# A gated-delta-net stage in a four-layer decoder kernel: projections in another order, PSUM banks given out by their last readers, weight parts given a higher rank

## The chip, the cores and the metric

The kernel runs on one core of a Trainium2 chip. The metric is the device time of one launch in microseconds (us).

## The reference, cut to what matters

A prompt of 512 tokens and 8 samples of 8 tokens (64 more) go through four layers: GLA, gated DeltaNet (GDN), S5, GLA. Each layer projects its input `x` (1024 wide), mixes over tokens with a recurrent state, gates with a SiLU branch, projects back and applies a LayerNorm to the residual sum. The change lies in the second layer:

```python
def gdn_mixer(x, w_in, w_conv, a_log, dt_bias, norm_g, w_out, conv0, s0):
    h = jnp.einsum('bld,de->ble', x, w_in).astype(F32)
    qkv, z, a, b = jnp.split(h, [...], axis=-1)
    ext = jnp.concatenate([conv0.astype(F32), qkv], axis=1)
    conv = ext[:, 0:L] * wc[0]
    for t in range(1, GDN_CONV):
        conv = conv + ext[:, t:t + L] * wc[t]
    q, k, v = jnp.split(jax.nn.silu(conv), [GDN_KW, 2 * GDN_KW], axis=-1)
    q = l2_normalize(...) * GDN_DK ** -0.5
    k = l2_normalize(...)
    g = -jnp.exp(a_log) * jax.nn.softplus(a + dt_bias)
    o, s = gdn_chunked(q, k, v, g, jax.nn.sigmoid(b), s0)
    o = rms_head(o, norm_g) * jax.nn.silu(z.reshape(bt, L, GDN_HEADS, GDN_DV))
    out = jnp.einsum('ble,ed->bld', o.reshape(bt, L, GDN_VW), w_out)
```

`gdn_chunked` needs only q, k and the gates for its scores and its triangular solve; v enters after the solve, z after the heads' outputs. There are 8 heads of width 128; the kernel works on pairs of heads, p = 0 to 3.

## The kernel before, in words

**The order is made by a planner in the kernel's own Python.** The code is written as threads (generators), each with a rank: low goes first. Every engine call is recorded (`record`, line 254) with its dependencies and a modelled cost (`cost`, 328). `run` (548) advances a model clock; on each engine it issues, of the operations that are ready in the model, the one of lowest rank (`issue`, 385). The order of issue is the program's order on that engine. On the chip each engine works through this order strictly, with real waits.

**Ranks.** The dense thread (all projections, in one list) has rank 10. What reads a finished projection out of PSUM has rank 1. Mixers have 3 and more: the thread of head pair p has 3 + p, its scores 2.5 + p, its heads 3 + p, its sample part 4.5 + p. Weight splitting has rank 5.

**Weights.** A unit of weights is 128 x 1024 words (512 KB), loaded by one SyncE DMA into one of RAW = 3 buffers (`load_weights`, 668). `split_weights` (687) makes a high part (a cast, on ScalarE or VectorE) and a low part (a VectorE subtraction) in one of RING = 4 buffers (line 142); a unit that is projected by `fm` (735) costs 48 matmuls of 288 columns: 8 slices of K, 2 token halves, 3 products of high and low parts. `prefetch` (681) splits a unit only when fewer than 4 units are held ahead of the dense thread, and when its load has landed.

**The dense thread** (`dense`, 705) takes the units strictly in the order of its list. `gdn_items` (1296) gives it for the GDN layer: the gates' unit and k, q of pair 0 (five units), then by line 1330

```python
        for w in 'v0 k1 k2 k3 v1 z0 z1 z2 v2 v3 z3'.split():
```

where `kN` is four units (k and q of two heads) and `vN`, `zN` are two. The out-projection (8 units, `out_items`, 827) follows; then the S5 layer.

**What a unit needs before its first matmul.** PSUM: `fm` takes two neighbouring banks of the eight (`bank(2)`, 465). SBUF: for a k, q or v unit `gdn_space` (1335) allocates 600 + 597 + 27 words a partition of convolution room, and a k unit (for itself and its q) 1024 words, a v unit 512, a z unit 576 (`gdn_zspace`, 1349). The pool has 32,960 words a partition. The dense thread must also leave `self.reserve` = 2500 words free (1301), a pair's thread 2000 until the pair before it is wholly done (1305). A thread that doesn't get its room waits, and with the dense thread all units behind it.

**After a k, q or v unit**, `gdn_conv` (1419): two copies out of PSUM, a scaling on ScalarE, three VectorE multiply-adds of 600 columns, one DMA of the convolution's last rows to `out_conv`, two SiLUs. After a z unit: one ScalarE SiLU of 576 columns.

**A pair** (`gdn_pair`, 1458) waits until pair p - 1 has passed its scores and pair p - 2 its solve; then scores (transposes, squares, matmuls, `gdn_scores`, 1632), one DMA to the scratch `scr`, a solve in 31 dependent VectorE steps (`gdn_solve`, 1615) that ends with one VectorE stream transpose, the heads (`gdn_head`, 1676; each ends with a DMA to `out_p_gdn` and waits for its v on the way), and the gate (`gate`, 1289), which waits for z, multiplies and hands the pair's output to the out-projection. A pair gives back its k, q, v and score buffers at the ends of its heads, its outputs and z only behind the gate.

**Banks.** `bank` takes the first free bank by its model time; a bank counts as free from `free` (489) on, that is once the reading instruction has been recorded, whether it has been issued or not. `bank_free` holds the model time of that call.

Of the kernel before, what the change touches and what calls it, by code (L numbers as in the profile page):

```python
# [184 lines left out]
class Core:  # L185
# [142 lines left out]
    def cost(self, op, method, args, kw, outs, ins):  # L328

        eng = op.eng  # L330
        column = any(v.shape[-1] == 1 for v in ins) or len(outs) > 1
        if not outs:
            op.cost, op.table = 1.28, args[0]
            return
        out = outs[0]
        size = lambda v: prod(v.shape[1:])
        n = size(out) if eng == 'PE' else max(size(v) for v in outs + ins)
        if eng == 'PE':
            m = 0.111 * size(ins[0]) / P
            if method == 'transpose':  # L340
                op.cost = max(n * 0.867e-3, 0.06)
            elif kw['lhsT'].dtype == F32R:
                op.cost = max(8e-3 + n * 0.434e-3, m)
            else:
                op.cost = 2 * max(n * 0.843e-3, m, 0.055)
        elif eng == 'DVE':
            in_ps = any(v.tensor.name == self.ps_name for v in outs + ins)
            op.cost = 0.07 + n / 960.0 * (0.5 if not in_ps and method in ('tensor_copy', 'tensor_scalar') else 1)
            if column:
                op.cost += 0.06  # L350
        elif eng == 'ACT':
            sb = all(v.tensor.name != self.ps_name for v in ins)
            op.cost = 0.05 + 0.835e-3 * n + (0.043 if sb else 0.0) + (0.093 if column else 0.0)
            op.table = ACT_SETS.get(args[2] if len(args) > 2 else None)
        elif eng == 'POOL':
            op.cost = 0.3 + 0.165 * n if kw.get('op') == ALU.pow else 0.12 + 2.2e-3 * n
            if method == 'memset':
                op.cost = 0.1 + 0.6e-3 * n
        else:
            run = min(self.run_of(v) for v in outs + ins)  # L360
            op.cost, op.tail = 0.45, prod(out.shape) / run * (8e-3 + 0.188e-3 * run) / 16
# [23 lines left out]
    def issue(self, op):  # L385
        e = op.eng
        t = max(self.now, op.ready)
        if e == 'PE' and not self.granted(t):
            op.cost *= 2
            self.pending[e] += op.cost / 2  # L390
        if op.table is not None:
            sets = op.table if isinstance(op.table, tuple) else (op.table,)
            if self.table not in sets:
                self.table = sets[0]
                if isinstance(op.table, tuple):
                    t += 1.28
        self.clock[e] = t + op.cost
        op.end = t + op.cost
        if e == 'SP':
            self.dma = max(self.dma, op.end + 0.7) + op.tail  # L400
            op.end = self.dma + 1.0
        op.issued = True
        self.pending[e] -= op.cost
        if e == 'PE' and op.rank >= 10:
            self.dense_backlog -= 1
        fn, args, kw = op.call
        fn(*args, **kw)  # L407
        op.call = None
        for s, lat in op.succ:
            s.ready = max(s.ready, t if lat is None else op.end + lat)  # L410
            s.pend -= 1
            if not s.pend:
                heappush(self.queue[s.eng][0], (s.ready, s.seq, s))
        op.succ = None

    def writers(self, *aps):
        ids = set()
# [46 lines left out]

    def bank(self, n=1, held=None):

        while True:
            best = None
            for b in range(0, 8, n):
                if held is not None and all({c, c + 1} & {b, *held} for c in range(0, 8, 2)):  # L470
                    continue
                if not any(self.banks[b:b + n]):
                    t = max(max(self.bank_free[b:b + n]), self.now)
                    key = (t, not self.banks[b ^ 1] if n == 1 else 0)
                    if best is None or key < best[0]:
                        best = (key, b)
            if best is None:
                yield BLOCK
                continue
            b = best[1]  # L480
            self.banks[b:b + n] = [True] * n
            if held is not None:
                held.append(b)
            v = self.ps[:, 512 * b:512 * (b + n)]
            return v if n == 1 else v.rearrange("p (a n) -> p a n", a=n)

    bank_free = [0.0] * 8

    def free(self, *aps):
        for v in aps:  # L490
            if v.tensor.name == self.ps_name:
                b, n = v.offset // 512, prod(v.shape[1:]) // 512
                self.banks[b:b + n] = [False] * n
                self.bank_free = list(self.bank_free)
                self.bank_free[b:b + n] = [self.now] * n
            else:
                off = v.offset
                n = self.used.pop(off)
                self.holes.append([off, n])
                self.holes.sort()  # L500
                merged = []
                for o, s in self.holes:
                    if merged and merged[-1][0] + merged[-1][1] == o:
                        merged[-1][1] += s
                    else:
                        merged.append([o, s])
                self.holes = merged
        self.frees += 1
# [39 lines left out]
    def run(self):  # L548
        while True:
            wake = []  # L550
            moved = True
            while moved:
                moved, wake = False, []
                for th in list(self.threads):
                    c = self.can_go(th)
                    if c is not True:
                        if c is not False:
                            wake.append(c)
                        continue
                    self.cur = th  # L560
                    moved = True
                    try:
                        v = next(th[0])
                    except StopIteration:
                        self.threads.remove(th)
                        continue
                    if v is BLOCK:
                        v = self.frees
                    elif isinstance(v, bass.AP):
                        v = self.writers(v)  # L570
                    elif isinstance(v, list):
                        v = self.writers(*v)
                    th[3] = v
                for e in ENGINES:
                    waiting, ready = self.queue[e]
                    while waiting and waiting[0][0] <= self.now + 1e-9:
                        _, s, op = heappop(waiting)
                        heappush(ready, (op.rank, s, op))
                    if ready and self.clock[e] <= self.now + 1e-9:
                        self.issue(heappop(ready)[2])  # L580
                        moved = True
# [15 lines left out]
class Kernel(Core):  # L597
    def __init__(self, ctx, tc, a, o, layers):
# [22 lines left out]
        self.reserve = 0  # L621
        self.xres = {}
        self.loaded = self.split = self.done = 0
        self.flat = []


    def load(self, dst, name, src=None):
# [53 lines left out]
    def prefetch(self, limit=1):  # L681
        self.load_weights(RAW)
        while limit and self.split < min(self.loaded, self.done + RING) and self.written(self.raw[self.split % RAW]):
            self.split_weights()
            limit -= 1

    def split_weights(self):
        cur, self.cur = self.cur, [None, 5] + self.cur[2:]
        src, lowrank = self.flat[self.split]
        raw, wh, wl = self.raw[self.split % RAW], self.wh[self.split % RING], self.wl[self.split % RING]  # L690
        for cs in self.pieces(self.split):
# [8 lines left out]
            else:  # L700
                self.TT(l, r, h.bitcast(F32), ALU.subtract)
        self.cur = cur
        self.split += 1

    def dense(self, items):

        for srcs, body in items:
            need = self.done + len(srcs)
            while self.split < need:
                self.prefetch(8)  # L710
                if self.split < need:
                    if self.split == self.loaded:
                        yield [self.raw[self.split % RAW]]
                    self.split_weights()
            idx = [i % RING for i in range(self.done, need)]
            ws = [(self.wh[i], self.wl[i]) for i in idx]
            for v in body(ws):
# [109 lines left out]
    def out_items(self, layer, wname):  # L827
# [9 lines left out]
        def half0(ws):  # L837
            ps, held = {}, []
            for u in range(4):
# [4 lines left out]
                for t in order:  # L844
# [6 lines left out]
                    if u == 3:  # L851
                        self.go(self.out_evac(layer, st, t, 0, ps[t]), 1)
                self.done += 1

        def half1(ws):
            for t in order:
                ps = yield from self.bank()
                for kt in range(KT):
# [3 lines left out]
                    if kt % 2:  # L862
                        yield
                        self.done += t == 3
                self.go(self.out_evac(layer, st, t, 1, ps), -1 if t == 3 and layer == self.layers - 1 else 0)

        w = self.a[wname]
# [428 lines left out]
    def gdn_items(self, layer):  # L1296
# [30 lines left out]
            return [([], body)]  # L1327

        items = [([], begin), self.fm_first(layer, first[:3])] + fms(first[3:])
        for w in 'v0 k1 k2 k3 v1 z0 z1 z2 v2 v3 z3'.split():  # L1330
            p = int(w[1])
            items += fms(kq(p)) if w[0] == 'k' else {'v': v, 'z': z, 'g': gate}[w[0]](p)
        return items
# [1017 lines left out]
```

## Time and profile before

| | us |
|---|---|
| median of 3 runs | 1349.48 |
| lowest and highest run | 1342.3, 1353.95 |
| the profiled execution | 1351.13 |
| its span, first to last instruction | 1349.3 |
| mean granted clock of TensorE in the span | 0.974 |

Nearly all instructions go through one recording line (407), so the profile shows no lines of the source; an instruction is told by its engine, operation, shape and buffers: `fx` is the fixed buffer (x and split weights), `sb` the working memory, `ps` PSUM. A matmul `ps<-fx` of 128x288 is a projection by `fm`; of 128x512 one of an out-projection. `ps<-sb` is mixer work. `PE` is TensorE, `DVE` VectorE, `ACT` ScalarE, `SP` SyncE, which issues the DMAs. A clock of 1.00 is 2.4 GHz, 0.5 is 1.2 GHz. By the weight loads the first GLA layer ends and GDN begins at about 300 us; GDN ends at about 750, S5 at about 1050.

### The profile page before, as it was taken

The page shows a single profiled execution, that of the slowest core. Times are in us where ns is not written, and L with a number is a line of the kernel's source. Part 1 is how long each engine was busy: PE and PEld are TensorE (multiplying, and loading weights), DVE is VectorE, ACT ScalarE, POOL GpSimd, SP SyncE. Part 2 cuts the span into 40 slices and gives each one's busy share as a digit, 9 for nine tenths or more (in the row PEclk, how much of TensorE's full clock was granted, in tenths as well). Part 3 has the DMA queues.
Part 4 walks back from the last instruction along what each step waited for, and adds up shares of the span by engine and source line. Part 5 has one row for each costly group of instructions (what it writes and reads, how often), then busy time and mean ns, then how long its engine had stood idle before and what let it go on. Part 6 is the DMA issues. An engine that isn't in the chain of part 4 may idle for free. (4 is left out here: it accounts for less than half of the span.)

```text
span 1349.3 us, 23532 instructions
## 1 busy us (share of the span) xinstructions
PE 1269.1 (94%) x8795; PEld 1185.0 (88%) x8795; DVE 960.1 (71%) x2099; ACT 599.2 (44%) x1329; POOL 152.6 (11%) x303
## 2 busy tenths in 40 slices
PE   8899999998998785999999989999999999999997
PEld 8898889778997685999977989899998899999986
DVE  5897887899999698786667729255334876655557
ACT  5553444423957663644541324235213245443430
POOL 5510010011111130121101000000000200000001
PEclk9999999999998897999989999899999999999999
DMA  7236444725367626263463697854325333332341
GB/s 237 67 114 207 145 161 149 244 86 173 105 171 225 173 68 182 86 180 107 120 206 102 250 264 199 227 147 106 95 87 176 113 111 99 129 130 98 121 152 70
DMA packets 129537, 198.35 MB, mean 147 GB/s; under 512 B 47176, under 2 KB 85960, under 8 KB 127376
## 3 DMA queue, kind: packets, MB, share of 16 engines
q1 hardware_dynamic: 129424, 196.86, 48.2%
q8 instruction: 69, 1.13, 0.4%
q14 instruction: 44, 0.36, 0.1%
HBM read 153.64 MB, written 47.37 MB: 149 GB/s over the span
## 5 line engine op out<-in xcount | busy, mean ns | idle before, releaser
L407 PE MATMUL ps<-fx 128*128 128x288 f32 (+2 forms) x6736 | 1053.6, 313 | 17.4 <-DVE sb L407 10.3
L407 PEld LDWEIGHTS ps<-fx 128*128 128x128 f32 x6736 | 953.9, 191 | 67.0 <-DVE sb L407 9.0
L407 DVE TENSOR_TENSOR fx<-sb,fx 128x1024 fp32r<-128x1024 f32 (+5 forms) x308 | 252.9, 847 | 168.2 <-ACT fx L407 164.6
L407 ACT CAST fx<-sb 128x1024 fp32r<-128x1024 f32 (+5 forms) x311 | 222.3, 741 | 314.0 <-PE ps L407 263.7
L407 PE MATMUL ps<-sb 128*128 128x128 f32 (+10 forms) x2059 | 301.0, 295 | 54.6 <-ACT sb L407 22.0
L407 PEld LDWEIGHTS ps<-sb 128*128 128x128 f32 (+7 forms) x2059 | 249.2, 177 | 88.7 <-ACT sb L407 28.6
L407 DVE TENSOR_TENSOR sb<-sb 128x128 f32<-128x128 f32 (+29 forms) x667 | 265.5, 415 | 13.9 <-ACT sb L407 4.8
L407 ACT COPY sb<-ps 128x512 f32<-128x512 f32 (+9 forms) x240 | 94.5, 413 | 132.8 <-PE ps L407 68.0
L407 DVE SCALAR_TENSOR_TENSOR sb<-sb 128x600 f32<-128x600 f32 (+6 forms) x205 | 134.0, 662 | 15.2 <-POOL sb L407 6.6
L407 ACT ACTIVATE sb<-sb 128x128 f32<-128x128 f32 (+9 forms) x240 | 108.1, 501 | 64.0 <-DVE sb L407 61.7
L407 DVE SCALAR_TENSOR_TENSOR sb<-sb,ps 128x256 f32<-128x256 f32 (+3 forms) x216 | 92.9, 458 | 59.3 <-PE ps L407 46.2
L407 POOL TENSOR_TENSOR sb<-sb 128x1 f32<-128x1 f32 (+4 forms) x46 | 73.5, 1602 | 426.2 <-DVE sb L407 371.9
L407 ACT ACTIVATE sb<-ps 128x128 f32<-128x128 f32 (+2 forms) x176 | 67.0, 384 | 83.7 <-DVE sb L407 42.9
L407 DVE SCALAR_TENSOR_TENSOR sb<-ps,sb 128x128 f32<-128x128 f32 (+3 forms) x112 | 55.6, 505 | 39.0 <-PE ps L407 36.5
L407 DVE COPY sb<-ps 128x256 f32<-128x256 f32 (+6 forms) x92 | 34.7, 379 | 59.6 <-PE ps L407 38.4
L407 POOL COPY sb<-sb 128x24 f32<-128x24 f32 (+4 forms) x92 | 29.7, 344 | 330.6 <-DVE sb L407 163.5
L407 ACT ACTIVATE sb<-ps,sb 128x128 f32<-128x128 f32 (+2 forms) x95 | 39.3, 436 | 30.0 <-PE ps L407 23.8
L407 ACT CAST fx<-ps 128x512 fp32r<-128x512 f32 (+2 forms) x32 | 17.5, 549 | 78.7 <-PE ps L407 75.0
L407 POOL MEMSET sb<- 128x3 f32 (+10 forms) x96 | 28.9, 317 | 192.9 <-DVE sb L407 139.1
L407 ACT ACT_TABLE_LOAD x31 | 39.8, 1283 | 1.2 <-PEq L2340 0.7
L407 POOL CAST fx<-sb 128x32 fp32r<-128x32 f32 (+1 forms) x33 | 9.8, 325 | 219.0 <-PE ps L407 219.0
L407 ACT COPY sb<-sb 32x288 f32<-32x288 f32 (+3 forms) x40 | 23.7, 606 | 10.7 <-DVE sb L407 7.4
(25 smaller groups left out, 254.5 us busy)
## 6 DMA issues: line engine op xcount, KB each, us to landing
sb<-in_gla_v SPq DMA_DIRECT2D x16, 512.0 KB, 4.0
sb<-in_gla_r SPq DMA_DIRECT2D x16, 512.0 KB, 3.7
sb<-in_gla_s SPq DMA_DIRECT2D x8, 1024.0 KB, 6.2
out_s_gla<-sb SPq DMA_DIRECT2D x8, 1024.0 KB, 4.3
sb<-in_gla_out SPq DMA_DIRECT2D x16, 512.0 KB, 3.9
sb<-in_gdn_s SPq DMA_DIRECT2D x32, 256.0 KB, 3.3
sb<-in_s_glu SPq DMA_DIRECT2D x16, 512.0 KB, 3.6
xres<-sb SPq DMA_DIRECT2D x12, 512.0 KB, 2.8
```

The source lines that it names most:

```text
L407: fn(*args, **kw)
```

## The change

1. The list of GDN projections has another order. Behind the first five units, `k1 v0 z0 k2 v1 z1 k3 v2 z2 v3 z3` takes the place of `v0 k1 k2 k3 v1 z0 z1 z2 v2 v3 z3`. The units, their loads and all that follows from each are the same.
2. A bank is given out only when every operation recorded on it has been issued (`cleared`), the earliest in model time first; until then the thread waits.
3. Splits of the unit that the dense thread needs now and of the next one get rank 2 in place of 5, ahead of all mixers (`hurry`, `promote`; called by `dense` and, in the out-projection, after each unit).
4. The planner's costs: accumulating ScalarE instructions 0.1 us more; GpSimd powers 0.1 more, its other operations 0.15 + 1.2 ns per column in place of 0.12 + 2.2, its memsets 0.08 + 0.86 ns in place of 0.1 + 0.6; the end of a DMA is taken 1 us later. These change no instruction, only the order.

```diff
@@ -351,11 +351,12 @@
         elif eng == 'ACT':
             sb = all(v.tensor.name != self.ps_name for v in ins)
             op.cost = 0.05 + 0.835e-3 * n + (0.043 if sb else 0.0) + (0.093 if column else 0.0)
+            op.cost += 0.1 if len(outs) > 1 else 0.0
             op.table = ACT_SETS.get(args[2] if len(args) > 2 else None)
         elif eng == 'POOL':
-            op.cost = 0.3 + 0.165 * n if kw.get('op') == ALU.pow else 0.12 + 2.2e-3 * n
+            op.cost = 0.4 + 0.165 * n if kw.get('op') == ALU.pow else 0.15 + 1.2e-3 * n
             if method == 'memset':
-                op.cost = 0.1 + 0.6e-3 * n
+                op.cost = 0.08 + 0.86e-3 * n
         else:
             run = min(self.run_of(v) for v in outs + ins)
             op.cost, op.tail = 0.45, prod(out.shape) / run * (8e-3 + 0.188e-3 * run) / 16
@@ -398,7 +399,7 @@
         op.end = t + op.cost
         if e == 'SP':
             self.dma = max(self.dma, op.end + 0.7) + op.tail
-            op.end = self.dma + 1.0
+            op.end = self.dma + 2.0
         op.issued = True
         self.pending[e] -= op.cost
         if e == 'PE' and op.rank >= 10:
@@ -412,6 +413,15 @@
             if not s.pend:
                 heappush(self.queue[s.eng][0], (s.ready, s.seq, s))
         op.succ = None
+
+    def promote(self, ops, rank):
+
+        for op in ops:
+            if not op.issued and op.rank > rank:
+                op.rank = rank
+                ready = self.queue[op.eng][1]
+                if any(q is op for _, _, q in ready):
+                    heappush(ready, (rank, op.seq, op))
 
     def writers(self, *aps):
         ids = set()
@@ -464,35 +474,41 @@
 
     def bank(self, n=1, held=None):
 
-        while True:
+        def choice():
             best = None
             for b in range(0, 8, n):
                 if held is not None and all({c, c + 1} & {b, *held} for c in range(0, 8, 2)):
                     continue
                 if not any(self.banks[b:b + n]):
-                    t = max(max(self.bank_free[b:b + n]), self.now)
-                    key = (t, not self.banks[b ^ 1] if n == 1 else 0)
-                    if best is None or key < best[0]:
-                        best = (key, b)
+                    t = self.cleared(b, n)
+                    if t is not None:
+                        key = (max(t, self.now), not self.banks[b ^ 1] if n == 1 else 0, b)
+                        best = key if best is None else min(best, key)
+            return best
+
+        while True:
+            best = choice()
             if best is None:
-                yield BLOCK
+                yield lambda: choice() is not None
                 continue
-            b = best[1]
+            b = best[2]
             self.banks[b:b + n] = [True] * n
             if held is not None:
                 held.append(b)
             v = self.ps[:, 512 * b:512 * (b + n)]
             return v if n == 1 else v.rearrange("p (a n) -> p a n", a=n)
 
-    bank_free = [0.0] * 8
+    def cleared(self, b, n):
+
+        ids = {i for e in ENGINES for i in self.bank_op[e][:, b:b + n].ravel().tolist()} - {-1}
+        ops = [self.ops[i] for i in ids]
+        return max((q.end for q in ops), default=0.0) if all(q.issued for q in ops) else None
 
     def free(self, *aps):
         for v in aps:
             if v.tensor.name == self.ps_name:
                 b, n = v.offset // 512, prod(v.shape[1:]) // 512
                 self.banks[b:b + n] = [False] * n
-                self.bank_free = list(self.bank_free)
-                self.bank_free[b:b + n] = [self.now] * n
             else:
                 off = v.offset
                 n = self.used.pop(off)
@@ -576,6 +592,8 @@
                     while waiting and waiting[0][0] <= self.now + 1e-9:
                         _, s, op = heappop(waiting)
                         heappush(ready, (op.rank, s, op))
+                    while ready and ready[0][2].issued:
+                        heappop(ready)
                     if ready and self.clock[e] <= self.now + 1e-9:
                         self.issue(heappop(ready)[2])
                         moved = True
@@ -621,7 +639,7 @@
         self.reserve = 0
         self.xres = {}
         self.loaded = self.split = self.done = 0
-        self.flat = []
+        self.flat, self.parts, self.soon = [], {}, 0
 
 
     def load(self, dst, name, src=None):
@@ -684,8 +702,15 @@
             self.split_weights()
             limit -= 1
 
+    def hurry(self, unit):
+
+        self.soon = max(self.soon, unit)
+        for i in [i for i in self.parts if i <= unit]:
+            self.promote(self.parts.pop(i), 2)
+
     def split_weights(self):
-        cur, self.cur = self.cur, [None, 5] + self.cur[2:]
+        cur, self.cur = self.cur, [None, 2 if self.split <= self.soon else 5] + self.cur[2:]
+        first = len(self.ops)
         src, lowrank = self.flat[self.split]
         raw, wh, wl = self.raw[self.split % RAW], self.wh[self.split % RING], self.wl[self.split % RING]
         for cs in self.pieces(self.split):
@@ -700,6 +725,7 @@
             else:
                 self.TT(l, r, h.bitcast(F32), ALU.subtract)
         self.cur = cur
+        self.parts[self.split] = self.ops[first:]
         self.split += 1
 
     def dense(self, items):
@@ -712,6 +738,7 @@
                     if self.split == self.loaded:
                         yield [self.raw[self.split % RAW]]
                     self.split_weights()
+            self.hurry(need)
             idx = [i % RING for i in range(self.done, need)]
             ws = [(self.wh[i], self.wl[i]) for i in idx]
             for v in body(ws):
@@ -851,6 +878,7 @@
                     if u == 3:
                         self.go(self.out_evac(layer, st, t, 0, ps[t]), 1)
                 self.done += 1
+                self.hurry(self.done + 1)
 
         def half1(ws):
             for t in order:
@@ -862,6 +890,7 @@
                     if kt % 2:
                         yield
                         self.done += t == 3
+                        self.hurry(self.done + 1)
                 self.go(self.out_evac(layer, st, t, 1, ps), -1 if t == 3 and layer == self.layers - 1 else 0)
 
         w = self.a[wname]
@@ -1327,7 +1356,7 @@
             return [([], body)]
 
         items = [([], begin), self.fm_first(layer, first[:3])] + fms(first[3:])
-        for w in 'v0 k1 k2 k3 v1 z0 z1 z2 v2 v3 z3'.split():
+        for w in 'k1 v0 z0 k2 v1 z1 k3 v2 z2 v3 z3'.split():
             p = int(w[1])
             items += fms(kq(p)) if w[0] == 'k' else {'v': v, 'z': z, 'g': gate}[w[0]](p)
         return items
```

## Rows read from the trace of the kernel before

**Rows 1.** The page, part 1: busy us, share of the span, instructions.
```profile
PE 1269.1 (94%) x8795; PEld 1185.0 (88%) x8795; DVE 960.1 (71%) x2099; ACT 599.2 (44%) x1329; POOL 152.6 (11%) x303
```

**Rows 2.** Windows: length, PE, PEld, DVE, ACT, POOL busy, PE clock, DMA share, GB/s.
```profile
350.00:400.00 50.00, 49.18 (x359) 47.83 (x358) 45.95 (x136) 37.02 (x95) 7.11 (x36) 1.00 0.49 127
400.00:450.00 50.00, 40.08 (x260) 37.61 (x259) 44.77 (x127) 38.04 (x94) 12.56 (x34) 0.89 0.85 225
450.00:500.00 50.00, 42.61 (x306) 38.01 (x305) 42.05 (x151) 29.43 (x108) 10.35 (x21) 0.97 0.34 95
500.00:550.00 50.00, 34.38 (x227) 31.99 (x226) 39.92 (x107) 22.75 (x55) 5.07 (x13) 0.80 0.59 155
550.00:600.00 50.00, 48.83 (x386) 46.60 (x385) 39.47 (x117) 30.08 (x103) 9.98 (x16) 1.00 0.53 148
...
950.00:1000.00 50.00, 50.00 (x377) 50.00 (x376) 15.77 (x16) 10.92 (x12) 0.00 (x0) 1.00 0.28 84
```

**Rows 3.** Waits of PE in the span: total us, times, longest.
```profile
PE ps L407 <- DVE sb L407: 24.6, 21, 3.9
...
PE ps L407 <- DVE fx L407: 5.4, 10, 1.6
PE ps L407 <- DMA sb<-Ud: 5.1, 2, 3.1
```

**Rows 4.** Windows, only instructions on fx: columns as in rows 2.
```profile
300.00:400.00 100.00, 87.97 (x621) 84.53 (x620) 20.43 (x20) 17.88 (x20) 0.00 (x0) 0.98 0.48 139
446.00:480.00 34.00, 0.41 (x3) 0.44 (x4) 1.64 (x2) 1.04 (x1) 0.00 (x0) 0.90 0.57 151
480.00:550.00 70.00, 38.84 (x216) 34.07 (x214) 8.11 (x9) 3.15 (x3) 0.00 (x0) 0.85 0.45 118
```

**Rows 5.** Timeline of SP, 399 to 696: start us, us, instruction.
```profile
399.40 0.38 SPq L407 DMA_DIRECT2D out_conv<-sb  x1
...
438.58 0.34 SPq L407 DMA_DIRECT2D scr<-sb  x1
...
484.71 0.38 SPq L407 DMA_DIRECT2D out_p_gdn<-sb  x1
...
516.87 0.38 SPq L407 DMA_DIRECT2D out_conv<-sb  x1
...
530.71 0.38 SPq L407 DMA_DIRECT2D out_conv<-sb  x1
...
547.27 0.38 SPq L407 DMA_DIRECT2D out_conv<-sb  x1
...
565.15 0.33 SPq L407 DMA_DIRECT2D scr<-sb  x1
...
576.42 0.41 SPq L407 DMA_DIRECT2D out_p_gdn<-sb  x1
...
695.28 0.38 SPq L407 DMA_DIRECT2D out_p_gdn<-sb  x1
```

**Rows 6.** Timeline of DVE: the solves' ends and the last gate.
```profile
442.09 0.72 DVE L407 STREAM_TRANSPOSE sb<-sb 128x288 f32<-128x288 f32 x1
...
495.00 0.72 DVE L407 STREAM_TRANSPOSE sb<-sb 128x288 f32<-128x288 f32 x1
...
616.85 0.74 DVE L407 STREAM_TRANSPOSE sb<-sb 128x288 f32<-128x288 f32 x1
...
704.21 0.82 DVE L407 SCALAR_TENSOR_TENSOR sb<-ps,sb 128x576 f32<-128x576 f32 x1
```

**Rows 7.** Timeline of ACT: the first SiLU of a z unit.
```profile
560.55 0.64 ACT L407 ACTIVATE sb<-ps 128x576 f32<-128x576 f32 x1
```

**Rows 8.** Timeline of PE, 506 to 515, with idle before and releaser.
```profile
506.66 0.53 PE L407 MATMUL ps<-fx 128*128 128x288 f32 x2
...
513.66 1.57 PE L407 MATMUL ps<-fx 128*128 128x288 f32 x5 [3.92 <-DVE sb L407]
```

**Rows 9.** DVE groups, 300 to 550: low parts of weights.
```profile
L407 DVE TENSOR_TENSOR fx<-sb,fx 128x1024 fp32r<-128x1024 f32 x25 | 30.4, 1218 | 1.1 <-ACT fx L407 1.1
```

## The prediction

> **What bounds the kernel now.** First the page's busy times: PE is busy 94% of the span, VectorE 71%, the others below half [rows 1]. The kernel is a PE kernel with holes, so the next view is the one that shows where the holes are. In the windows of 50 us I read two losses: idle time (50 less the PE's busy time) and, because at a granted clock of 0.5 matmuls take twice as long, 50 x (1 - clock) as an upper bound for the clock. At 350 to 400 that is 0.8 + 0 us, at 550 to 600 1.2 + 0. Between them lie 9.9 + 5.5 = 15.4 (400 to 450), 7.4 + 1.5 = 8.9 (450 to 500) and 15.6 + 10.0 = 25.6 (500 to 550): 50 us in 150, all inside the GDN layer [rows 2]. A stretch of nothing but projections runs without a loss, 377 matmuls in 50 us, 0.133 us each, so 48 of them, one unit, take 6.4 us [rows 2].
>
> The third view asks whether projections were lacking there. From 300 to 400 the fixed buffer fed 621 matmuls, 12.9 units, 7.7 us each. From 446 to 480 it fed 3. From 480 to 550 it fed 216, 4.5 units, 15.6 us each [rows 4]. So PE stands still because the dense thread does. By the code it can lack weights, banks or room in SBUF. Weights were there: only one low part's worth of VectorE time (1.6 us) falls into 446 to 480, because the ring of four was full and nothing drew from it [rows 4]. Room fits best: 17 units are through, the next is the second k of pair 3, which wants 2250 words and leaves 2500 over, while pairs 0 and 1 both hold their scores. Projections start again as pair 0's heads end (the second is out at 484.7 [rows 5]), which is when a pair gives its buffers back.
>
> The fourth view shows what comes late by that. Pair 1's solve ends at 495.0 [rows 6], but its v convolutions are out only at 530.7 and 547.3, and its second head only at 576.4 [rows 5]. From the solve's end that is 81 us; pair 0 took 42.6 (442.1 to 484.7), its v being early [rows 5, 6]. Pair 0's z is ready at 560.6 [rows 7], 76 us after its heads; until then its outputs stay in SBUF and pair 1 has to leave 2000 words free.
>
> **The change part by part.** *The order.* No unit, load, cast, convolution or DMA is added or taken away; all of a unit's instructions move with it, its load and its `out_conv` DMA on SP and two copies on GpSimd among them. By unit 17 the new list has done v0, k0 to k2 and z0 where the old one has v0, k0 to k2 and half of k3. z0 stands there 10 units earlier, v1 comes as units 18 and 19 in place of 20 and 21, z1 as 20 and 21 in place of 24 and 25; k3 goes from 16 to 19 back to 22 to 25. Room at unit 17 is about the same (two z of 576 for a k of 1024 and its samples), so I expect the stop before 480 to stay. What changes is behind it. Pair 1's heads get v about when their solve ends; pair 0's gate runs right after its heads. In exchange pair 3's scores wait for k3.
>
> That makes a chain to the last gate, now at 704.2 [rows 6]. Restart at 480, then eight units of P us to the last q of pair 3, then from row to row: last matmuls of a unit to its convolution's DMA 9.7 (507.2 to 516.9 [rows 5, 8]); convolution to `scr` 39.2 as in pair 1 (399.4 to 438.6; pair 3 itself took 48.3, in the crowded stretch) [rows 5]; `scr` to the end of the solve 51.7 (565.2 to 616.9 [rows 5, 6]); solve to second head 42.6, as pair 0; head to gate 8.9 (695.3 to 704.2 [rows 5, 6]). Sum: 632.1 + 8 P. With P = 6.4, PE's bare speed, 683.3, a gain of 21 us; with 7.7, the pace of 300 to 400, 693.7, a gain of 10; with 15.6, the pace of 480 to 550, 756.9, a loss of 53. The order breaks even at P = 9.0. I take P = 7.0, midway between the first two: VectorE had 46 of 50 us to do at 350 to 400, 40 at 500 to 550 [rows 2], and two of the eight units are z, which cost VectorE one 1.22 us low part [rows 9] and no convolution. That is 688.1: **-16 us**. PE itself allows it: from 450 to 600 it loses 35.7, and with the 1.0 per window of the quiet stretches it would lose 3 [rows 2], so the most there is to gain is 33. v3 (units 30 and 31, as before) is then done at 480 + 14 x 7 = 578, ahead of pair 3's solve, so nothing new stands in front of the heads.
>
> *Rank 2 for the next unit's parts.* PE waits 5.4 us in all for low parts [rows 3]; I take 4 of them. In 400 to 450 VectorE is busy 44.8 of 50 us [rows 2], and low parts of rank 5 stand behind mixers there; of the 15.4 us lost I take 2, because an earlier projection brings its convolution to the same full engine. Together **-6** (from 0 to -15). The price: 1.22 us of VectorE per unit [rows 9] go ahead of the pair that sets the end. Of the chain's 142 us behind k3 (39.2 + 51.7 + 42.6 + 8.9) some 17 units could pass at 8 us each, 21 us if none passed now; but they pass now too, only later in the queue. **+2** (0 to 21). A low part that waits for its cast would also hold VectorE, but over 25 of them that was 1.1 us [rows 9].
>
> *Banks.* In the model a thread could take a bank whose readers stood far back in a queue, with another one empty. On the chip that is a projection that waits for a copy out of PSUM: the 3.92 us at 513.7 [rows 8]. Of 24.6 us that PE waits for VectorE's writes to SBUF [rows 3] I can't tell which are such; bounds 0 and -12 (half), taken **-3**. What can be late next: a projection needs two neighbouring banks clear at one moment, and threads of lower rank number can take each as it clears. The Trainium skill (TensorE: Matmul & The Clock Gate, "A second HAM failure mode: psum-queue depth-cycling") says that a PE that idles briefly between groups while it goes round the banks can fall back in clock. Rows speak against it here: 350 to 400 goes round the banks with 0.8 us of idle at a clock of 1.00, and the clock falls where idle runs to 15.6 us in 50 [rows 2]. By the rows this costs nothing; by the rule it is the fourth rival.
>
> *Costs.* No operation changes. The DMA's later end moves readers of fresh loads back: PE waits 5.1 us for the S5 inputs [rows 3], so between -5 and, where a reader then comes too late, +5; **-1**.
>
> Sum: -16 - 6 + 2 - 3 - 1 = -24 us. The profiled execution took 1351.1 (span 1349.3 and 1.8 around it), which makes 1327. The median is 1.7 lower than that execution, far less than the 11.7 between the fastest and the slowest run, so I leave it at **1327**.
>
> **The rivals.** *PE-bound to the end (1306).* Early v and z free SBUF so much sooner that 450 to 600 becomes like its neighbours: -33 in place of -16, and 400 to 450 gives another 4 by its splits; 1351 - 24 - 17 - 4 = 1306. For it: VectorE has 80% to do at 500 to 550, so nothing but order stands in the way. Against it: the solve is serial and took 52 us.
>
> *The pairs set the pace (1344).* If P stays at 7.7 (-10), the splits get in the mixers' way (+6) and the rest gives its low ends (-3), it is -7. For it: VectorE at 92% in 350 to 400; against it: pair 1's 81 us from solve to head, which aren't VectorE's.
>
> *k3 comes too late (1367), the slower side.* One mechanism: the stop for room repeats, at v1 to k3, now that z0, v1 and z1 lie in SBUF before k3; P stays between the two measured paces. From P = 9.0 on the order loses. At P = 12 the last gate comes at 728.1, +24; with -8 from the other parts the time is 1351 + 16 = 1367. For it: 15.6 us a unit is what was measured behind the stop. Against it: in that stretch pair 1's heads waited for v1, which here stands first.
>
> *Projections starved of bank pairs (1369).* There are 107 bodies that take two banks (17 in each GLA, 33 in GDN, 32 in S5, 8 for v). If one in ten waits another 3.92 us [rows 8] and the clock keeps, that is +42; 1327 + 42 = 1369. For it is the rule above, against it the same idle times at 350 to 400.
>
> **How the numbers follow.** Forecast 0.42 (its own range 1315 to 1340), PE-bound 0.25, the pairs' pace 0.17, k3 too late 0.12, bank pairs 0.04. A measurement of this kernel can tell about 1% from no change, here 1336 and 1363. Faster: nearly nine tenths of the forecast's share, all of the PE-bound and a tenth of the third, 0.64. Slower: the last two, 0.16. The rest is 0.20. The range 1294 to 1362 leaves out some 0.04 below, for parts that add up better than in the PE-bound case, and some 0.13 above.
>
> **What would show it.** Right: no stretch of 30 us without a projection, or one that ends with a pace near 7 us a unit; pair 1's second head some 45 us behind its solve; pair 0's z SiLU before 450; the last gate near 690; PE's loss in 400 to 600 near 25. Waits of PE for VectorE's writes to `fx` near 1. Wrong: k3's convolutions after 560 and the last solve after 640; more and shorter waits in S5 and the last GLA, which the order doesn't touch, would speak for the banks; a gain outside GDN above 10 us would mean that I gave banks or costs too little.

## The result and the profile after

The changed kernel takes 1305.88 us (median of 4 runs, 1302.93 to 1309.08), against 1349.27 before. The ratio is 0.9683, with a 95% interval from 0.9635 to 0.9731: 3.2% faster. The profiled execution took 1305.55, its span is 1303.7, so it lies where the median lies.

The page, part 1, of the changed kernel, answers to [rows 1]:

```profile
PE 1255.2 (96%) x8795; PEld 1175.5 (90%) x8795; DVE 964.5 (74%) x2117; ACT 599.9 (46%) x1317; POOL 164.6 (13%) x303
```

PE runs the same 8795 instructions in 45.6 us less of span; its busy time fell by 13.9, with the mean granted clock up from 0.974 to 0.986. The windows of the GDN layer answer to [rows 2] (length, PE, PEld, DVE, ACT, POOL busy, PE clock, DMA share, GB/s):

```profile
300.00:350.00 50.00, 49.83 (x376) 48.66 (x375) 47.28 (x122) 32.64 (x61) 10.77 (x28) 1.00 0.45 147
350.00:400.00 50.00, 46.25 (x337) 44.63 (x336) 47.89 (x134) 35.86 (x89) 10.75 (x31) 1.00 0.67 190
400.00:450.00 50.00, 46.55 (x327) 44.08 (x327) 46.12 (x138) 28.65 (x77) 12.85 (x28) 0.90 0.77 205
450.00:500.00 50.00, 44.85 (x329) 40.91 (x330) 44.49 (x147) 36.49 (x119) 10.62 (x21) 0.97 0.30 85
500.00:550.00 50.00, 47.56 (x342) 46.08 (x341) 44.98 (x127) 31.59 (x91) 5.46 (x14) 0.93 0.66 173
550.00:600.00 50.00, 48.82 (x387) 46.84 (x386) 44.62 (x122) 26.83 (x79) 13.26 (x28) 1.00 0.60 166
600.00:650.00 50.00, 48.77 (x406) 47.36 (x405) 38.88 (x113) 26.07 (x83) 9.31 (x14) 1.00 0.37 111
650.00:700.00 50.00, 49.95 (x243) 40.73 (x242) 39.90 (x88) 15.28 (x37) 6.92 (x11) 1.00 0.57 183
```

Read as in the prediction, idle plus 50 x (1 - clock): 400 to 600 loses 8.5 + 6.6 + 5.9 + 1.2 = 22.2 us, where it lost 51.1. From 650 to 700, the window of the last pair's tail, the loss is 0.05; before it was 2.68 + 3.5 = 6.2, by the last of these rows of the kernel before:

```profile
300.00:350.00 50.00, 46.45 (x327) 44.34 (x326) 47.40 (x125) 27.34 (x46) 6.79 (x27) 0.97 0.46 152
600.00:650.00 50.00, 50.00 (x406) 49.10 (x405) 35.70 (x93) 22.74 (x54) 6.43 (x18) 1.00 0.40 113
650.00:700.00 50.00, 47.32 (x328) 44.02 (x327) 30.20 (x84) 25.50 (x87) 5.44 (x5) 0.93 0.56 176
```

The other windows from 300 on nearly cancel: 4.9 us less are lost at 300 to 350, 2.9 and 1.2 more at 350 to 400 and 600 to 650. From 300 to 700 the loss goes from 63.1 to 27.4, by 35.7 us, and the last gate came 36.7 us earlier. The windows of instructions on `fx` alone answer to [rows 4]:

```profile
446.00:480.00 34.00, 5.04 (x30) 3.99 (x30) 1.63 (x2) 1.12 (x1) 0.00 (x0) 0.95 0.41 110
480.00:550.00 70.00, 46.40 (x281) 39.95 (x282) 11.93 (x13) 5.82 (x6) 0.00 (x0) 0.95 0.53 144
```

The stop is still there: 30 matmuls on `fx` between 446 and 480, and none for 24.3 us (35.4 before). Behind it 281 come where 216 came. The timeline of SP answers to [rows 5]: the last convolutions of k3 (559.4) and v3 (625.7), pair 1's second head (520.1), pair 3's scores (573.5) and second head (656.5):

```profile
520.07 0.50 SPq L408 DMA_DIRECT2D out_p_gdn<-sb  x1
...
559.40 0.38 SPq L408 DMA_DIRECT2D out_conv<-sb  x1
...
573.50 0.34 SPq L408 DMA_DIRECT2D scr<-sb  x1
...
625.73 0.38 SPq L408 DMA_DIRECT2D out_conv<-sb  x1
...
656.46 0.40 SPq L408 DMA_DIRECT2D out_p_gdn<-sb  x1
```

The timeline of DVE answers to [rows 6]: pair 1's solve ends at 471.5, pair 3's at 616.0, and the last gate starts at 667.5.

```profile
471.52 0.71 DVE L408 STREAM_TRANSPOSE sb<-sb 128x288 f32<-128x288 f32 x1
...
615.96 0.74 DVE L408 STREAM_TRANSPOSE sb<-sb 128x288 f32<-128x288 f32 x1
...
667.46 0.82 DVE L408 SCALAR_TENSOR_TENSOR sb<-ps,sb 128x576 f32<-128x576 f32 x1 [0.18 <-PE ps L408]
```

This is the line to look at twice. The end of pair 3's solve hasn't moved: 616.85 before [rows 6], 615.96 after. What moved is what stands behind it: 88 us from the solve's end to the last gate's end before, 52 after. And v3, which the heads of pair 3 need, was in before only at this time (SP of the kernel before):

```profile
661.47 0.38 SPq L407 DMA_DIRECT2D out_conv<-sb  x1
```

It stands at the same place of the list in both kernels (units 30 and 31) and came 35.7 us earlier, because the projections ahead of it did.

PE's waits answer to [rows 3]:

```profile
PE ps L408 <- DVE sb L408: 20.0, 20, 3.7
...
PE ps L408 <- DVE fx L408: 1.3, 1, 1.3
...
PE ps L408 <- DMA sb<-Ud: 0.4, 1, 0.4
```

### The profile page after: what moved, and what is told of

Its sections match the earlier page's. It is cut to its first block, busy times and chain, and to the rows that moved or that the text cites. A ratio compares the mean times of both kernels' runs of the same rounds, so it can differ in the third digit from the quotient of the medians.

```text
span 1303.7 us, 23541 instructions
## 1 busy us (share of the span) xinstructions
PE 1255.2 (96%) x8795; PEld 1175.5 (90%) x8795; DVE 964.5 (74%) x2117; ACT 599.9 (46%) x1317; POOL 164.6 (13%) x303
## 4 chain that ended last, share of the span: by engine, by line
PE 62%; DVE 22%; DMA 6%; ACT 4%; issue 4%; POOL 1%; SPq 1%; POOLq 0%; DVEq 0%; ACTq 0%
PE ps L408 62%; DVE sb L408 18%; DVE fx L408 4%; ACT sb L408 3%; DMA sb<-Ud 2%; POOL sb L408 1%; ACT L408 1%; ACT fx L408 1%; SPq L408 1%; DMA s5Kx<-s5K 1%; DMA sb<-in_gdn_s 0%; DMA sb<-scr 0%; DMA sb<-in_rst 0%; DMA sb<-s5Kx 0%; DMA sb<-in_gla_q 0%
## 5 line engine op out<-in xcount | busy, mean ns | idle before, releaser
L408 PE MATMUL ps<-sb 128*128 128x128 f32 (+10 forms) x2059 | 292.7, 292 | 32.3 <-DVE sb L408 17.7
L408 PEld LDWEIGHTS ps<-sb 128*128 128x128 f32 (+6 forms) x2059 | 244.3, 175 | 61.9 <-DVE sb L408 20.4
L408 DVE TENSOR_TENSOR sb<-sb 128x128 f32<-128x128 f32 (+26 forms) x667 | 263.9, 414 | 13.5 <-ACT sb L408 3.9
L408 ACT COPY sb<-ps 128x512 f32<-128x512 f32 (+10 forms) x233 | 91.8, 411 | 120.6 <-PE ps L408 66.0
L408 ACT ACTIVATE sb<-sb 128x128 f32<-128x128 f32 (+10 forms) x239 | 108.9, 504 | 72.7 <-DVE sb L408 63.6
L408 DVE SCALAR_TENSOR_TENSOR sb<-sb 128x512 f32<-128x512 f32 (+7 forms) x205 | 133.5, 660 | 10.2 <-POOL sb L408 7.4
L408 DVE COPY sb<-ps 128x256 f32<-128x256 f32 (+8 forms) x99 | 37.8, 388 | 51.0 <-PE ps L408 32.5
L408 POOL COPY sb<-sb 128x24 f32<-128x24 f32 (+4 forms) x92 | 40.2, 460 | 237.6 <-DVE sb L408 138.5
L408 ACT ACTIVATION_READ_ACCUMULATOR sb<-ps 128x1 f32 x136 | 27.2, 200 | 0.1
```

## The experiments

No kernel leaves out work. They differ in the order of issue, and in one more thing: for a copy or a cast the planner picks VectorE or ScalarE by what its model clocks show at that moment (`cp`, 632, and `split_weights`). So the plan also moves instructions between the two: 2099 on VectorE and 1329 on ScalarE before [rows 1], 2117 and 1317 in the change. What is said above of the costs, that they change no instruction, isn't quite so. Each ratio is to the kernel before on the same chip. The times of the solve, of v3's last convolution and of the last gate's end are from each run's one profiled execution, whose span is given with them (13 executions of the kernel before, on one chip, spread over 11.5 us, so a few us between two rows mean nothing); "rest" is the span less the last gate.

| run | ratio (95%) | span | pair 3's solve | v3's last conv. | last gate | rest |
|---|---|---|---|---|---|---|
| before | 1 | 1349.3 | 616.8 | 661.5 | 705.0 | 644.3 |
| the change | 0.9683 (0.9635 to 0.9731) | 1303.7 | 616.0 | 625.7 | 668.3 | 635.5 |
| e1 order alone | 0.9673 (0.9628 to 0.9719) | 1307.6 | 621.3 | 623.5 | 670.7 | 636.9 |
| e3 rank alone | 1.0019 (0.9995 to 1.0044) | 1351.1 | 636.7 | 651.7 | 694.0 | 657.1 |
| e5 all but the order | 0.9814 (0.9787 to 0.9840) | 1319.2 | 610.5 | 642.4 | 675.1 | 644.1 |
| e6 all but the costs | 0.9825 (0.9793 to 0.9856) | 1319.8 | 637.2 | 631.1 | 685.0 | 634.8 |
| e7 v1 ahead of k3 | 0.9905 (0.9873 to 0.9936) | 1333.8 | 602.2 | 644.1 | 684.9 | 648.9 |
| e8 z0 behind v0 | 0.9922 (0.9894 to 0.9950) | 1334.1 | 657.0 | 642.8 | 704.2 | 629.9 |
| e9 reserve 1000 | 1.0005 (0.9987 to 1.0023) | 1343.6 | 623.9 | 653.1 | 696.5 | 647.0 |
| e10 all but the rank | 0.9696 (0.9645 to 0.9747) | 1308.2 | 626.9 | 627.4 | 677.4 | 630.8 |
| e11 v1 and v2 early | 0.9893 (0.9835 to 0.9951) | 1334.6 | 615.0 | 645.5 | 681.0 | 653.6 |
| e12 order and costs | 1.0037 (1.0007 to 1.0068) | 1349.6 | 659.1 | 652.0 | 708.4 | 641.2 |
| e13 order and banks | 0.9833 (0.9755 to 0.9911) | 1320.7 | 632.6 | 632.1 | 675.0 | 645.7 |
| e14 k3 up, z1 behind | 0.9943 (0.9922 to 0.9965) | 1340.5 | 617.3 | 645.3 | 687.8 | 652.7 |

**One part at a time.** The order alone (e1) is one line on the kernel before:

```diff
-        for w in 'v0 k1 k2 k3 v1 z0 z1 z2 v2 v3 z3'.split():
+        for w in 'k1 v0 z0 k2 v1 z1 k3 v2 z2 v3 z3'.split():
```

> The kernel before with the new list of GDN projections alone. Theory A (v and z early free SBUF and the heads; the order carries the gain of the GDN layer): 1310 to 1328, the last gate near 670 to 690 in place of 704, pair 1's second head some 45 us behind its solve. Rival B (the planner's parts, banks, rank and costs, carry it): 1340 to 1350, the last gate near 700. Rival C (none works without the others): within 1% of the kernel before.

Measured: 1304.80 us. It brings all that the change brings, more than theory A had. Its windows (columns as above) show the same hole filled, 500 to 550 most of all, from 34.38 to 49.56:

```profile
400.00:450.00 50.00, 45.57 (x322) 44.70 (x323) 45.74 (x129) 31.85 (x83) 10.89 (x33) 0.97 0.79 228
450.00:500.00 50.00, 43.49 (x342) 38.34 (x342) 43.32 (x154) 30.10 (x112) 11.84 (x20) 1.00 0.42 124
500.00:550.00 50.00, 49.56 (x375) 47.06 (x373) 46.76 (x127) 33.60 (x98) 6.99 (x16) 1.00 0.63 174
```

The rank alone (e3) has `promote`, `hurry` and its calls, of the change's third part:

```diff
-        cur, self.cur = self.cur, [None, 5] + self.cur[2:]
+        cur, self.cur = self.cur, [None, 2 if self.split <= self.soon else 5] + self.cur[2:]
```

> The kernel before with rank 2 for the parts of this and the next weight unit alone. Theory A: 1343 to 1350 (PE's 5.4 us of waits for low parts go, little else). Rival B: 1325 to 1338, with PE's loss at 400 to 450 cut by half.

Measured: 1346.39, no difference. PE's waits for low parts went from 5.4 to 3.9 us only. The change with the old list of projections (e5):

```diff
-        for w in 'k1 v0 z0 k2 v1 z1 k3 v2 z2 v3 z3'.split():
+        for w in 'v0 k1 k2 k3 v1 z0 z1 z2 v2 v3 z3'.split():
```

> The changed kernel with the old list of GDN projections (banks, rank 2 and costs stay). Theory A: 1332 to 1346, the stretch without projections near 446 to 480 and pair 1's late v come back. Rival B: 1306 to 1318. Rival C: about 1349.

Measured: 1321.34. This falls between theory A and rival B: the planner's parts without the new list fill much of the same hole (last gate 675.1). What the prediction gives to the order came here without it: the stop falls apart into 8.1 and 11.4 us, and pair 1's second head is 39.4 us behind its solve (497.7 to 537.1). So the effects don't add up: -3.3% and -1.9% together give -3.2%, and beside the other three parts the new list is worth 1.3% (0.9683 against 0.9814). The change with the old costs (e6):

```diff
-            op.end = self.dma + 2.0
+            op.end = self.dma + 1.0
```

and the four cost lines above it likewise.

> The changed kernel with the old costs of the planner. Theory A: 1304 to 1312, no more than 5 us from the changed kernel, the difference in the S5 layer (750 to 860). Rival B (the later end of a DMA in the plan brings the 8 us that S5 gained): 1312 to 1318, PE's waits for DMAs in S5 back near 10 us.

Measured: 1323.09, worse than both had it, and not where both looked: the rest is 634.8, as in the changed kernel; the GDN layer is 17 us longer.

**Which place in the list.** Moves in the kernel before, one at a time:

```diff
-        for w in 'v0 k1 k2 k3 v1 z0 z1 z2 v2 v3 z3'.split():
+        for w in 'v0 k1 k2 v1 k3 z0 z1 z2 v2 v3 z3'.split():
```

> The kernel before with v1 moved two places, from behind k3 to ahead of it, all else in the old order. Theory V (pair 1's heads waited for v1, and what they held stopped the projections): most of the order's 40 us, 1312 to 1325, pair 1's second head near 535 in place of 576. Theory Z (pair 0's outputs, held for z0, and the 2000 words that pair 1 must leave until pair 0 is done): 1338 to 1348.

```diff
-        for w in 'v0 k1 k2 k3 v1 z0 z1 z2 v2 v3 z3'.split():
+        for w in 'v0 z0 k1 k2 k3 v1 z1 z2 v2 v3 z3'.split():
```

> The kernel before with z0 moved up behind v0, all else in the old order. Theory Z: most of the order's 40 us, 1312 to 1325, pair 0's gate near 490 in place of 562, the stretch without projections under 20 us. Theory V: 1340 to 1352, and pair 1's second head still near 576 or later, v1 being two units later.

Measured: 1334.64 and 1336.04. Both theories miss. With v1 early, pair 1's second head is out at 516.9 and pair 3's solve ends at 602.2, the earliest of all; the last gate is still at 684.9, with v3 at 644.1. With z0 early pair 0's gate runs at 479, but pair 3's solve ends at 657. Each is worth a quarter of the new list, or a little more. Then v1 and v2:

```diff
-        for w in 'v0 k1 k2 k3 v1 z0 z1 z2 v2 v3 z3'.split():
+        for w in 'v0 k1 k2 v1 k3 v2 z0 z1 z2 v3 z3'.split():
```

> The kernel before with v1 ahead of k3 and v2 right behind it, z0 to z3 as late as before. Theory V, now for pairs 1 and 2 (a pair stands when its v isn't there at its solve's end; v1 alone left pair 2 waiting 73 us for v2): 1312 to 1322, the second heads of pairs 1 and 2 near 40 us behind their solves. Rival (the z units' places carry the other half, by the outputs that are held for them): 1328 to 1338.

Measured: 1333.75, what the rival had. The heads of pairs 1 and 2 do follow their solves in 35 us each (483.6 to 519.0, 570.7 to 606.2), as theory V says, and it brings no more than v1 alone: v3, behind z0 to z2 as before, comes at 645.5 (644.1 with v1 alone).

**Whether the stop was for want of room.** In the kernel before:

```diff
-            self.reserve = 2500
+            self.reserve = 1000
```

> The kernel before, where the dense thread has to leave 1000 words of SBUF in place of 2500 in the GDN layer. Room theory (the stop at 446 to 479 is for want of SBUF): the stop begins at least one unit later or is under 15 us, the time 1325 to 1342, or longer if the pairs then lack the room. Rival (it lacks a bank pair or split weights): the stop stays at the same unit with some 35 us, 1343 to 1352.

Measured: 1346.91, no difference. By its own signs the room theory is missed: the stop begins behind the same 17 units, it lasts 15.7 us and not under 15, and the time lies in the rival's range. But the stop is much shorter (windows of instructions on `fx`; 47 matmuls where 3 stood, 268 where 216 stood [rows 4]):

```profile
446.00:480.00 34.00, 9.76 (x47) 6.83 (x47) 1.23 (x1) 2.23 (x3) 0.00 (x0) 0.90 0.50 141
480.00:550.00 70.00, 40.77 (x268) 37.73 (x268) 10.02 (x10) 5.56 (x6) 0.00 (x0) 0.90 0.56 147
```

The longest stretch without a projection goes from 35.4 to 15.7 us, by the one number of the reserve. So 20 us of the stop are for want of SBUF; what holds the other 15.7 isn't shown. Pair 1's solve then ends at 509.6 in place of 495.0. That may be for want of room, or because four convolutions now share VectorE with it (484.8 to 504.8, one before); no run tells the two apart. The next two windows of PE are short (same view as [rows 2]), the first less than before (41.48 for 34.38), the second more (44.60 for 48.83):

```profile
500.00:550.00 50.00, 41.48 (x286) 38.27 (x285) 41.29 (x117) 28.21 (x70) 6.38 (x13) 0.86 0.63 164
550.00:600.00 50.00, 44.60 (x326) 42.26 (x325) 39.51 (x126) 27.54 (x92) 9.07 (x16) 0.93 0.44 118
```

To shorten the wait that one sees gave nothing in the total.

**The planner's parts with the order.** The change without `hurry`, rank 5 for all parts (e10):

```diff
-            self.hurry(need)
```

and the rest of that part likewise.

> The changed kernel with rank 5 for all weight parts. If the rank brings its direct waits (some 4 us for low parts): 1308 to 1313. If the order alone fills the GDN layer: 1302 to 1309, PE's waits for low parts near 5 us again but not on the path. If it hinders the mixers: 1295 to 1302.

Measured: 1306.13. PE's waits for low parts are 1.4 us without the rank as they are 1.3 with it. The order with the costs (e12), and with the bank rule (e13), are the kernel before with these parts of the diff:

```diff
+            op.cost += 0.1 if len(outs) > 1 else 0.0
...
-            op.end = self.dma + 1.0
+            op.end = self.dma + 2.0
```

> The new order and the new costs, with the old banks and ranks. If the costs do something by themselves (the S5 layer's waits for DMAs): 1292 to 1300. If not: 1300 to 1310, as the order alone.

```diff
-                    t = max(max(self.bank_free[b:b + n]), self.now)
+                    t = self.cleared(b, n)
```

> The new order and the new rule for banks, with old ranks and costs. If the rule for banks takes what the costs gave back (order, banks and rank together were at 1323): 1318 to 1328. If it is the rank that does it: 1300 to 1310.

Measured: 1352.32 and 1323.06. e12 was expected by neither side: the costs, which change only the plan, take back all that the order gave. k3's last convolution is 34.5 us later than with the order alone (593.0, 558.5), pair 3's scores 33.2, its solve and the last gate 38: the delay goes whole down the chain of the prediction. The projections' stop is 31.5 us long, but that isn't what costs it: e10 has one of 32.6 us at 1306. The page, part 1, of e12, shows more instructions on VectorE and fewer on ScalarE than e1 has (2103 and 1325):

```profile
PE 1267.0 (94%) x8795; PEld 1182.9 (88%) x8795; DVE 967.0 (72%) x2125; ACT 593.2 (44%) x1304; POOL 167.7 (12%) x303
```

Whether this shift or the order of issue makes e12's delay isn't shown. The bank rule costs 1.7% on top of the order, and on top of order and costs it gains 3.4% (e10 against e12). The rank shows nothing in three comparisons: alone 1.0019, on order and banks 0.9825 against 0.9833, on order, banks and costs 0.9683 against 0.9696. The first excludes a gain of 4 us; the other two, with intervals of 0.3 to 0.8% to either side, can't tell 4 us (0.3%). There is no time for the bank rule alone or the costs alone: with either the planner comes to no order, because its threads block one another.

**Whether k3's place sets the end.** The new list, k3 two units earlier, z1 behind it, on the kernel before:

```diff
-        for w in 'v0 k1 k2 k3 v1 z0 z1 z2 v2 v3 z3'.split():
+        for w in 'k1 v0 z0 k2 v1 k3 z1 v2 z2 v3 z3'.split():
```

> The new order alone (old banks, ranks, costs), with k3 two units earlier and z1 behind it: k1 v0 z0 k2 v1 k3 z1 v2 z2 v3 z3. If k3's place sets the last gate (the chain of the prediction): pair 3's scores are out some 12 us earlier than the 579.7 of the new order alone, the last gate near 655, 1290 to 1300. If PE's and VectorE's work sets it: 1300 to 1310, the last gate near 670. If z1's delay holds room and so the projections: 1310 to 1330.

Measured: 1340.54. Pair 3's scores are out at 578.62 (579.73 with the order alone) and its solve ends at 617.33 (621.29). But this doesn't say that k3 is off the path, because the edit moved k3's place and not its time: its last convolution is at 561.25, in e1 at 558.55. From the restart behind 19 units, e1 has done k3's last unit with 288 projection matmuls at 555.0, e14 with 192 at 555.9 (groups on PE, e1 from 478.7 to 554.8, e14 from 483.2 to 555.6):

```profile
L407 PE MATMUL ps<-fx 128*128 128x288 f32 x288 | 46.4, 306 | 0.0
L407 PE MATMUL ps<-fx 128*128 128x288 f32 x192 | 32.3, 312 | 0.0
```

So the question that e14 was to settle stays open. The timelines of this run, SP and DVE:

```profile
561.25 0.38 SPq L407 DMA_DIRECT2D out_conv<-sb  x1
...
578.62 0.34 SPq L407 DMA_DIRECT2D scr<-sb  x1
...
645.35 0.38 SPq L407 DMA_DIRECT2D out_conv<-sb  x1
```

```profile
617.33 0.69 DVE L407 STREAM_TRANSPOSE sb<-sb 128x288 f32<-128x288 f32 x1
...
686.97 0.82 DVE L407 SCALAR_TENSOR_TENSOR sb<-ps,sb 128x576 f32<-128x576 f32 x1
```

Its z1 is in at 564 in place of 508, projections stop for 13.7 us at 523, between the two heads' units of k3, PE has 41.44 of 50 to do at 500 to 550, and v3 comes 21.8 us later than in e1. Two units of z1 ahead of k3 or behind it come with 17 us at the last gate (687.8 against 670.7); another 16 are lost behind it.

## Why the prediction was right, and where it was off

The direction, the layer and the signs in the trace were right, the size too small: 1327 forecast, 1305.9 measured, within the range and at the number of the rival "PE-bound to the end" (1306). That rival's account isn't met either: it let 450 to 600 lose 3 us, they lose 13.8 (6.6 + 5.9 + 1.2, and rounding), and about what it lacks there came behind the last gate. That the forecast came as near as it did is luck in good part: its main term is a sum whose errors cancel.

*The step that failed* is the pricing of the order's chain, "632.1 + 8 P", from the restart by way of k3's convolution and pair 3's scores to the last gate, and with it the claim that v3 would be done at 578, ahead of pair 3's solve. P was not 7.0. In the changed kernel the restart, at 473.6, comes behind unit 18; the seven units to the last q of pair 3 end at 555.6, 11.7 us each, and the thirteen to the last of v3 at 621.3, 11.4 each (groups of projections on PE, from 473.6 to 555.4 and to 621.15):

```profile
L408 PE MATMUL ps<-fx 128*128 128x288 f32 x336 | 54.4, 308 | 0.0
L408 PE MATMUL ps<-fx 128*128 128x288 f32 x624 | 98.5, 305 | 0.0
```

That is nearly the 12 of the rival "k3 too late", beyond the break-even of 9.0: with the other terms as I took them the last gate would have stood at 707.7 (555.6 + 9.7 + 39.2 + 51.7 + 42.6 + 8.9), later than before. But nearly all the other terms were too long: last matmul to convolution's DMA 3.8 (I took 9.7), on to `scr` 14.1 (39.2), to the end of the solve 42.5 (51.7), to the second head 40.5 (42.6), to the gate 11.0 (8.9). Against the forecast the restart gave -6.4 us, the units +26.0, these terms -40.2; that is 667.5 in place of 688.1. The largest miss, 39.2, was read in pair 1. In the seven runs with the new list or that of e14 (the change, e1, e6, e10, e12, e13, e14), pair 3's `scr` follows k3's last convolution in 14.0 to 21.5 us; with the old list, or one or two moves in it, in 23.9 or more. So in those seven the rows fit k3 as what the scores wait for; no run moved k3's time alone.

At the end of the chain a second thing arrives that the forecast had 58 us ahead of the solve's end (578 against 636.6) and that came 5 behind it: v3 (621.3 against 616.0). In hindsight, the later of v3's last convolution + 42 and pair 3's solve + 49 gives the last gate's end within 2 us in 11 of the 14 rows of the table, and 6 to 9 us too late in the other three (e5, e11, e13); the two numbers are read off these same runs. Before, that is 703.5 against 665.8: v3 sets it, with 38 us of slack in the solve. After, it is 667.7 against 665.0: both at once. Three rows have nearly the same solve (616.8, 617.3, 616.0: before, e14, the change); v3 is at 661.5, 645.3 and 625.7 there, and the last gate at 705.0, 687.8 and 668.3. But no run moves v3 alone. z3 comes with it, and the gate waits for z3 too: in the change and in the three rows that don't fit, the gate ends only 12 to 14 us behind z3's last SiLU, in all others 16 to 48. So that v3 was the bound is read off the runs, not shown.

*What was right in it.* The stop before 480 stayed (24.3 us, in place of 35.4), is for want of SBUF in part at least (e9), and z0 and v1 paid where they were said to: pair 0's SiLU at 390, pair 1's second head 48.6 us behind its solve (forecast 45), PE's loss of 400 to 600 22.2 us (forecast 25). That v alone isn't it, nor z alone, I hadn't seen: e7, e8 and e11 give a quarter to a third each, the list as a whole everything.

*The rank, -6 + 2.* Not seen in any comparison. PE's waits for low parts did fall to 1.3 us, as forecast, but e10 has 1.4 without the rank: they fell with the rest of the plan. None of the 4 us came to the total in e3, the one comparison that can tell so small a gain.

*Banks, -3, and costs, -1.* Neither has a size of its own: +1.7% and -3.4% for the one, +3.8% and -1.5% for the other, by what stands beside them. To sum parts was the wrong form for changes to a planner. The rival of the starved bank pairs, for which a rule of the Trainium skill (TensorE: Matmul & The Clock Gate, "A second HAM failure mode: psum-queue depth-cycling") spoke, did not come about as a whole: the change is faster, and its mean granted clock rose from 0.974 to 0.986. But the rise is not the bank rule's. Beside the order alone the rule cost 1.7%, and the mean granted clock of the profiled executions is 0.983 with it (e13) and 0.987 without (e1); whether starved pairs do that isn't shown.

*S5.* Behind the last gate 8.8 us were gained (644.3 to 635.5). In e6's expectation I looked for them in the DMA's later end, and PE's waits for S5 inputs did go, from these rows before, 10.7 us in all with the 5.1 of [rows 3]:

```profile
PE ps L407 <- DMA sb<-s5C: 2.4, 4, 1.0
PE ps L407 <- DMA sb<-s5Kx: 2.3, 2, 1.2
PE ps L407 <- DMA sb<-s5G: 0.9, 1, 0.9
```

to 1.5 after. But the rest is 636.9 in e1 and 634.8 in e6, both without the new costs and with 7.8 and 5.9 us of such waits. Over all runs the rest goes from 629.9 to 657.1, and no part of the change stands for that spread. What makes it stays open, as does what in the costs throws e12's plan off.

## What to carry to other kernels

Before a chain is priced, ask of each thing at its end how much slack it has: here v3, 31 units down an in-order list, was given 58 us and had none. A chain whose sum comes out near can be wrong in nearly every term; measure the terms one by one. A place in a list is not a time: before reading a run that moves a part up, see that the part came earlier (in e14 it didn't). A wait that is seen to be for want of a buffer need not be what costs: the stop shortened from 35.4 to 15.7 us gave nothing, and the order alone gave 3.3% with a stop of 20.0 us still there. Where a greedy planner makes the order, measure the parts in company and apart: the same cost lines were worth -1.5% beside one set of parts and +3.8% beside another, the same list 3.3% alone and 1.3% beside the other parts.
